# LRU gates in two matmul passes over blocks of 64 features, and attention gates earlier, in a hybrid decoder block

## The chip, the core and the metric

The kernel runs on one core of a Trainium2 chip. The core has a matrix engine (TensorE, in the profile PE), a vector engine (VectorE, DVE), a scalar engine for activation functions (ScalarE, ACT), a general engine (GpSimd, POOL) and SyncE (SP), whose queue here issues most transfers. Each engine runs its own instructions in order and waits for the others through semaphores. The metric is the time of one execution on the device in microseconds; less is better.

## The reference

One layer of a decoder block on 2048 positions of 1024 features, in float32. One projection gives everything: queries, keys and values of three groups of dilated attention, an attention gate, the input u_lru of a recurrent branch, its gate, and logits that merge both branches. The part that the change touches is the recurrent branch (RG-LRU) with its gates, which are block-diagonal: 16 blocks of 64 features, each with its own 64 x 64 matrix for r and for i.

```python
u = causal_depthwise_conv(u_lru, conv_w[l], conv_b[l])
...
xb = x.reshape(B, S, LRU_BLOCKS, LRU_BLOCK_WIDTH)
r = jax.nn.sigmoid((jnp.einsum('bsgi,gij->bsgj', xb, w_r).reshape(B, S, C) + b_r).astype(jnp.float32))
i = jax.nn.sigmoid((jnp.einsum('bsgi,gij->bsgj', xb, w_i).reshape(B, S, C) + b_i).astype(jnp.float32))
log_a = -LRU_C * r * jax.nn.softplus(-lam.astype(jnp.float32))
a = jnp.exp(log_a)
mult = jnp.sqrt(jnp.maximum(-jnp.expm1(2.0 * log_a), 0.0))
u = mult * (i * x.astype(jnp.float32))
...
_, h = lax.associative_scan(combine, (a, u), axis=1)
```

The attention's output is multiplied by silu(g_attn); silu(g_lru) multiplies h.

## The kernel before

**Stages.** The projection stage computes all projections together with rotary, the LRU branch and the gates, and stores the results in DRAM. Then come the attention stage, the combination of the groups, the output projections and the layer norm. Only the projection stage is touched.

**High and low parts.** A float32 value is kept as a high part in a rounded type (`F32R`, made by ACT with a copy) and the low rest (value minus high part, made by DVE or POOL). A product takes three matmul passes: high by high, high by low, low by high.

**Products and ticks.** The sequence is done in two halves of 1024 positions. In each half the list `seq` (line 534 on) gives 36 pairs of 128-feature tiles: `qk` (a key and a query tile), `ug` (LRU gate and LRU input), `v`, `ga` (attention gate), `mg` (merge gates). A pair is multiplied by a scheme with seven block products (the first pair of a half has eight plain ones). One product is 12 matmuls of 128x512 (`product`, line 590) and is one tick of the loop that writes out the instructions; a half has 8 + 35 x 7 = 253 ticks. Each engine's order is the order in which this loop writes. The raw weights, their sums, their high parts (L268) and low parts (L232) for a product are written three to four ticks ahead of it. In the first half DVE and POOL make the low parts and SP stores them in `wl_scr`; in the second half SP loads them back into the tiles `l` (`load_lo`, L290), of which there are four. A product's PSUM bank is one of four and is emptied by DVE or ACT (`evacuate`).

**Passage.** Shortly before the second half, x for its columns is loaded (`load_raw`, L226) by SP and combined on DVE, ACT and POOL (`comb`, `fourth`).

**Chains.** What follows a product runs as a chain, a generator that yields `Ask(...)` before each step. At each tick the loop steps every chain whose lag has passed, whose number of free tiles (`need` + `keep` of 32 slots) is there, and whose engines have budget left: a tick gives each engine 2.75 us, and an Ask's numbers (ACT=..., DVE=...) are taken off. So larger numbers in an Ask push later steps to later ticks. The chains: `qk_chain` (four swap transfers L310, products with cos and sin, their sum, for queries a split L333, stores L327, L338, L341), `v_chain` (four transposes on PE L358, a copy on ACT, store L370), `silu_chain` (two ACT, one DVE, L396 to L399; the attention gate is then stored, the LRU gate waits for h), `mg_chain`, and `lru`.

**The LRU chain** (`lru`, line 430) runs once per tile of 128 features (i, 8 of them) and chunk of 512 positions (c, 4 of them), 32 times. It does the convolution, and brings the gate weights twice per tile (`bring_gw`, 16 times): wr and wi as 128x128 block-diagonal matrices with two transfers into `gr` (L441, L442), then one high part on ACT (L459) and one low part on DVE. It splits v into vh and vl (L466 and L232), and has the six gate matmuls run in the middle of a later product (`pe_later`; L475 to L477: two banks `g`, three passes each). Two tanh (L488, L489) read the two banks; then follow exp, tanh, a square root, the products, the scan on DVE (L510), the product with the LRU gate on POOL and a store (L525). At most two chunks are between begin and scan (`gate["live"]`), and one between gates and tanh (`gate["busy"]`). For even i, chunk 1 is put off to the second half. So 12 chunks and 8 weight sets fall in the first half, 20 and 8 in the second.

**Order of the pairs.** The loop that makes `seq` takes from the list `light` (6 `v`, 2 `ga`, 6 `mg`): one behind an even tile's pair, two around an odd tile's.

## Time and profile before

| | |
|---|---|
| median of three runs | 2367.07 us (2362.84 to 2371.19) |
| profiled execution | 2367.64 us |
| its span, first to last instruction | 2365.8 us |
| granted TensorE clock, mean | 0.979 |
| PE, DVE, ACT, POOL busy | 95%, 73%, 46%, 43% |
| projection stage | 0 to 1546 us of the span |
| first half, second half | ticks 0 to 252, 253 to 505 |

How to read it: an engine's line such as `L605 PE MATMUL` names the kernel's line, the engine and the operation, then output<-input by tile names. A busy PE is an upper bound, because the records of neighbouring matmuls overlap. A wait is put down to the engine whose semaphore came last; `SPq` is SP's transfer queue. Line 232 is the helper `tt`, so the tile names tell what it does there. The program's built order, engine by engine, tells in which tick each instruction stands.

### The profile page before, as it was taken

How to read it: one execution, taken by the hardware profiler on the slowest of the kernel's cores; microseconds unless marked ns; L12 is line 12 of the kernel's file. 1: busy time of each engine (PE TensorE's matmuls, PEld its weight loads, DVE VectorE, ACT ScalarE, POOL GpSimd, SP SyncE). 2: the span in 40 equal slices, each digit the busy share in tenths (PEclk: the TensorE clock that was granted, in tenths of full speed). 3: DMA queues.
4: the chain of work that ended last, by engine and by line, in shares of the span. 5: the costliest groups of instructions: out<-in, count | busy, mean ns of one | idle time of the engine just before them, and what ended most of it. 6: DMA issues, size and time to landing. Idle time of an engine off the chain costs nothing.

```text
span 2365.8 us, 34610 instructions
## 1 busy us (share of the span) xinstructions
PE 2243.7 (95%) x11008; PEld 1878.5 (79%) x11008; DVE 1726.1 (73%) x3116; ACT 1084.9 (46%) x1977; POOL 1014.7 (43%) x760
## 2 busy tenths in 40 slices
PE   6999999999999799999999999989999999979998
PEld 4788888888788687787787877779999878758886
DVE  7888888899888676676667777546666558857677
ACT  4346445455465455465456665446666611121100
POOL 5554554456545433223232232368666326532220
PEclk8999999999999899999999999989999999999999
DMA  6888997988988987898897888897886579874431
GB/s 237 238 260 236 271 286 230 265 258 265 269 260 295 287 245 229 240 245 233 230 252 244 268 241 255 253 255 191 214 211 162 162 233 304 269 241 155 157 116 63
DMA packets 347174, 551.48 MB, mean 233 GB/s; under 512 B 99056, under 2 KB 140016, under 8 KB 342384
## 3 DMA queue, kind: packets, MB, share of 16 engines
q1 hardware_dynamic: 308160, 489.80, 66.2%
q0 software_dynamic: 20160, 36.71, 9.5%
q10 hardware_dynamic: 18672, 22.75, 3.1%
q8 instruction: 88, 1.44, 0.3%
q14 instruction: 94, 0.77, 0.1%
HBM read 343.81 MB, written 180.16 MB: 221 GB/s over the span
## 4 chain that ended last, share of the span: by engine, by line
PE 61%; DMA 13%; DVE 10%; issue 7%; POOL 4%; ACT 3%; SPq 2%; ACTq 0%; DVEq 0%; POOLq 0%
PE q L605 43%; DMA l<-wl_scr 4%; PE o L978 3%; PE s L939 2%; DMA A<-qh_scr 2%; PE pt L954 1%; PE yb L1167 1%; PE yb L1168 1%; PE yb L1166 1%; PE z L1260 1%; PE z L1258 1%; PE z L1259 1%; DVE xcB L232 1%; POOL C L789 1%; DMA wA<-in_w_in_dram 1%
## 5 line engine op out<-in xcount | busy, mean ns | idle before, releaser
L605 PE MATMUL q<-xT,hS 128*128 128x512 f32 x1680 | 523.3, 393 | 10.5 <-ACT hS L268 6.1
L605 PE MATMUL q<-xT,l 128*128 128x512 f32 x1120 | 438.9, 392 | 3.2 <-DVE l L232 3.2
L605 PE MATMUL q<-xB,hA 128*128 128x512 f32 x1248 | 398.7, 401 | 19.1 <-ACT hA L268 11.5
L605 PE MATMUL q<-xB,l 128*128 128x512 f32 x904 | 362.2, 401 | 36.8 <-DMA l<-wl_scr 28.2
L605 PEld LDWEIGHTS q<-xT,hS 128*128 128x128 f32 x1680 | 317.0, 189 | 78.7 <-ACT hS L268 7.1
L605 PEld LDWEIGHTS q<-xB,hA 128*128 128x128 f32 x1248 | 240.5, 194 | 70.6 <-ACT hA L268 12.3
L605 PEld LDWEIGHTS q<-xT,l 128*128 128x128 f32 x1120 | 211.7, 189 | 48.9 <-DVE l L232 4.3
L605 PEld LDWEIGHTS q<-xB,l 128*128 128x128 f32 x904 | 173.9, 192 | 81.4 <-DMA l<-wl_scr 35.1
L945 ACT ACTIVATE p<-p,osb 128x256 f32<-128x256 f32 (+1 forms) x384 | 156.5, 455 | 114.1 <-DVE osb L943 113.4
L232 POOL TENSOR_TENSOR sw<-sw,sin 128x512 f32<-128x512 f32 x96 | 159.8, 1681 | 98.6 <-DMA sw<-y 96.5
L943 DVE CUSTOM_DVE_ANT_0 p<-s,mask 128x256 f32<-128x256 f32 (+1 forms) x384 | 125.1, 364 | 100.4 <-PE s L939 59.6
L250 POOL DMA_DIRECT2D wS<-in_w_in_dram x140 | 123.8, 994 | 169.8 <-DMA wS<-in_w_in_dram 103.0
L268 ACT ACTIVATE hA<-wA 128x512 fp32r<-128x512 f32 x218 | 134.9, 623 | 95.3 <-DMA wA<-in_w_in_dram 51.1
L605 PE MATMUL q<-xB,hS 128*128 128x512 f32 x560 | 175.4, 394 | 2.1 <-DVE v L232 2.0
L605 PE MATMUL q<-xT,hA 128*128 128x512 f32 x560 | 174.1, 392 | 0.2 <-DVE u L232 0.2
L978 PE MATMUL o<-V,ptb 128*128 128x65 f32 x1200 | 165.0, 276 | 9.7 <-ACT ptb L959 7.8
L232 POOL TENSOR_TENSOR S<-S,wA 128x512 f32<-128x512 f32 x35 | 50.1, 1433 | 281.6 <-DVE S L232 116.3
L978 PEld LDWEIGHTS o<-V,ptb 128*128 128x128 f32 x1200 | 151.7, 194 | 21.4 <-ACT ptb L959 19.4
L232 DVE TENSOR_TENSOR y<-y,cos 128x512 f32<-128x512 f32 x96 | 121.3, 1267 | 48.6 <-DMA sw<-y 48.3
L232 POOL TENSOR_TENSOR l<-wA,hA 128x512 fp32r<-128x512 f32 x74 | 116.6, 1576 | 55.7 <-ACT hA L268 37.7
L1232 POOL TENSOR_TENSOR me<-gA,ybr 128x512 f32<-128x512 f32 x32 | 47.8, 1507 | 180.1 <-DVE gA L1231 177.6
L605 PEld LDWEIGHTS q<-xB,hS 128*128 128x128 f32 x560 | 104.3, 189 | 24.8 <-issue 2.9
(190 smaller groups left out, 4995.2 us busy)
## 6 DMA issues: line engine op xcount, KB each, us to landing
wA<-in_w_in_dram SPq DMA_DIRECT2D x218, 256.0 KB, 5.6
wl_scr<-l SPq DMA_DIRECT2D x105, 512.0 KB, 4.9
l<-wl_scr SPq DMA_DIRECT2D x105, 512.0 KB, 6.2
wS<-in_w_in_dram SPq DMA_DIRECT2D x140, 256.0 KB, 4.9
wS<-in_w_in_dram POOLq DMA_DIRECT2D x140, 256.0 KB, 7.0
sw<-y SPq DMA_DIRECT2D x384, 64.0 KB, 3.7
mg_scr<-y SPq DMA_DIRECT2D x59, 256.0 KB, 5.9
o_scr<-osb ACTq DMA_DIRECT2D x48, 264.0 KB, 5.9
```

The lines of the kernel that those rows point to most:

```text
L232: eng.tensor_tensor(out=out, in0=in0, in1=in1, op=op)
L250: pool.dma_start(t, w_part(s, x), accum_op=ALU.add)
L268: act.activation(h, r, AF.Copy)
L605: pe.matmul(bank, w[:, ks], x[:, kk, xx], start=(first and i == 0), stop=(last and i == 11))
L789: pool.tensor_tensor(out=b2[hs, h, t], in0=flat(b2[hs, h, t]), in1=flat(B1[hs, h, t]), op=ALU.subtract)
L939: pe.matmul(s[:, h, (0 if g == 2 and n else lo):256], q, k, start=(i == 0), stop=(i == 1))
L943: dve.tensor_tensor_reduce(out=p[:, h, lo:256], in0=s[:, h, lo:256], in1=mask[:, lo:256], scale=1.0, scalar=3e38, op0=ALU.add, op1=ALU.min ...
L945: act.activation(p[:, h, lo:256], p[:, h, lo:256], AF.Exp, scale=-1.0, bias=mm)
L954: pe.transpose(pt[:, 2 * h + x, :], p[:, h, x * P:(x + 1) * P], ident)
L978: pe.matmul(o[:, n % 2, h * 65:h * 65 + 65], ptb[:, 2 * h + x, :], V[:, kb, vo + h * 65:vo + h * 65 + 65], start=(x == lo // P), stop=(x = ...
L1166: pe.matmul(yb, WL[f][:, 0, k], xx[:, 0], start=(k == 0), stop=False)
L1232: pool.tensor_tensor(out=ME[c][:, f], in0=ga, in1=yb, op=ALU.add)
```

## The change

A tile of 128 features holds two gate blocks, b = 0 (rows 0 to 63) and b = 1 (rows 64 to 127). The changed kernel forms one matmul operand per block: the block's high part on its own rows and its low part on the other 64 rows of the same tile. So the first tile, still named vh, holds high and low of block 0, and vl holds those of block 1. The weights for block b have r and i beside each other in the 128 columns and the same 64 rows twice, below each other; a second such set holds their low parts. One pass with the high weights gives high by high plus high by low, a second pass with the low weights adds low by high (and low by low, which the kernel before left out). So a chunk has four gate matmuls instead of six. Bank 0 then has r and i of block 0 on its two halves, bank 1 has i and r of block 1, and each tanh becomes two of 64 partitions; the one for i moves its rows to the other half.

The pieces on ACT and DVE change so: the split of v from one to two instructions on each engine, a weight set from one to four on each, the tanh from two to four on ACT. The transfers of a weight set become four, of the 64x64 blocks alone (16 KB each), instead of two of 64 KB. Three Asks name larger numbers. In `light`, the two attention gate pairs come to the first and the fourth place instead of the seventh and eighth.

```diff
@@ lru, weights' transfers @@
-            sp.dma_start(gr[:, 0:P], a["wr"][i])
-            sp.dma_start(gr[:, P:2 * P], a["wi"][i])
+            for b, names in ((0, ("wr", "wi")), (1, ("wi", "wr"))):
+                for k, n in enumerate(names):
+                    rows = slice(64 * b, 64 * b + 64)
+                    sp.dma_start(gr[rows, 64 * k:64 * k + 64], a[n][i, rows, rows])
...
@@ weights' parts @@
-            yield Ask(ACT=.4, DVE=.4, lag=2, need=1, keep=1)
+            yield Ask(ACT=.9, DVE=.9, lag=2, need=1, keep=1)
             w = GW[i] = take("gw" + nm)
-            act.activation(w[:, 0:2 * P], gr[:, 0:2 * P], AF.Copy)
-            tt(dve, w[:, 2 * P:], gr[:, 0:2 * P], flat(w[:, 0:2 * P]), ALU.subtract)
+            for b in range(2):
+                rows, cols = slice(64 * b, 64 * b + 64), slice(2 * P * b, 2 * P * b + P)
+                low = slice(2 * P * b + P, 2 * P * b + 2 * P)
+                for o in (rows, slice(64 - 64 * b, P - 64 * b)):
+                    act.activation(w[o, cols], gr[rows, 0:P], AF.Copy)
+                    tt(dve, w[o, low], gr[rows, 0:P], flat(w[rows, cols]), ALU.subtract)
...
@@ split of v @@
-        gw = GW[i].rearrange("p (l j f) -> p l j f", l=2, j=2)
-        yield Ask(need=2, keep=1, ACT=.66, DVE=.75)
+        gw = GW[i].rearrange("p (b l f) -> p b l f", b=2, l=2)
+        yield Ask(need=2, keep=1, ACT=1.3, DVE=1.5)
         vh, vl = take("vh" + nm), take("vl" + nm)
-        act.activation(vh, v, AF.Copy)
-        tt(dve, vl, v, flat(vh), ALU.subtract)
+        for b, t in enumerate((vh, vl)):
+            rows, other = slice(64 * b, 64 * b + 64), slice(64 - 64 * b, P - 64 * b)
+            act.activation(t[rows], v[rows], AF.Copy)
+            tt(dve, t[other], v[rows], flat(t[rows]), ALU.subtract)
...
@@ gate matmuls @@
-                pe.matmul(g, gw[:, 0, j], vh, start=True, stop=False)
-                pe.matmul(g, gw[:, 0, j], vl, start=False, stop=False)
-                pe.matmul(g, gw[:, 1, j], vh, start=False, stop=True)
+                for l in range(2):
+                    pe.matmul(g, gw[:, j, l], (vh, vl)[j], start=(l == 0), stop=(l == 1))
...
@@ tanh @@
-        yield Ask(lag=2, need=3, keep=1, ACT=3.3, DVE=.75)
+        yield Ask(lag=2, need=3, keep=1, ACT=4.7, DVE=.75)
...
-        act.activation(tr, pg[0], AF.Tanh, scale=0.5, bias=brh[:, 0, i:i + 1])
-        act.activation(ti, pg[1], AF.Tanh, scale=0.5, bias=brh[:, 1, i:i + 1])
+        for t, k in ((tr, 0), (ti, 1)):
+            for b in range(2):
+                rows = slice(64 * b, 64 * b + 64)
+                src = rows if k == 0 else slice(64 - 64 * b, P - 64 * b)
+                act.activation(t[rows], pg[b][src], AF.Tanh, scale=0.5, bias=brh[rows, k, i:i + 1])
...
@@ order of the light pairs @@
-    light += [("ga", FT_GA + 2 * j, FT_GA + 2 * j + 1) for j in range(2)] + mg[2:]
+    for j in range(2):
+        light.insert(3 * j, ("ga", FT_GA + 2 * j, FT_GA + 2 * j + 1))
+    light += mg[2:]
```

## The prediction

> **What bounds the kernel now.** I read the page's first part, then busy time by stages, then what TensorE waited for in each stage, and then single instructions.
>
> ```profile
> span 2365.8 us, 34610 instructions
> PE 2243.7 (95%) x11008; PEld 1878.5 (79%) x11008; DVE 1726.1 (73%) x3116; ACT 1084.9 (46%) x1977; POOL 1014.7 (43%) x760
> ```
>
> The change touches the projection stage alone, so I cut the span there: the start, the first half of the sequence, the passage between the halves, the second half, and the rest (attention and output, untouched). Columns: window, its length, busy time and count of each engine, granted clock, DMA share, GB/s.
>
> ```profile
> 0.00:77.30 77.30, 50.51 (x169) 37.86 (x169) 59.75 (x83) 30.70 (x52) 39.72 (x38) 0.87 0.69 226
> 77.30:777.10 699.80, 696.60 (x3109) 574.15 (x3110) 610.93 (x721) 350.37 (x585) 374.16 (x275) 1.00 0.89 264
> 777.10:813.70 36.60, 23.50 (x85) 18.34 (x84) 23.12 (x28) 14.78 (x26) 15.65 (x12) 0.77 0.83 241
> 813.70:1546.10 732.40, 703.64 (x3073) 575.35 (x3072) 499.11 (x664) 404.45 (x660) 218.92 (x174) 0.98 0.86 247
> 1546.10:2365.80 819.70, 769.45 (x4577) 672.78 (x4575) 533.24 (x1623) 284.60 (x654) 366.21 (x263) 0.98 0.66 195
> ```
>
> In the first half PE is busy for 696.6 of 699.8 us while VectorE (DVE) has 610.9, or 87%: PE is the bound there and DVE is close behind. In the second half PE lacks 28.8 us. TensorE's own waits, asked for 130 to 700 us (first two rows), 700 to 820 and 820 to 1500, give the reasons:
>
> ```profile
> PE q L605 <- ACT hi L332: 1.6, 1, 1.6
> PE q L605 <- DVE v L232: 0.9, 2, 0.8
> ...
> PE q L605 <- ACT hA L268: 11.0, 1, 11.0
> ...
> PE q L605 <- DMA l<-wl_scr: 25.7, 13, 3.5
> ```
>
> So nearly nothing in the first half, one wait of 11 us in the passage, and 13 waits for the low weight parts coming back from memory in the second half. The gates appear in no wait of PE: their matmuls stand inside a product and cost their own time.
>
> **Term 1: 64 matmuls go.** The end of one product with the gates of one chunk in its middle, from the timeline of PE:
>
> ```profile
> 1307.48 0.39 PE L475 MATMUL g<-vh,gw 128*128 128x512 f32 x1
> 1307.71 0.39 PE L476 MATMUL g<-vl,gw 128*128 128x512 f32 x1
> ...
> 1308.84 0.61 PE L605 MATMUL q<-xT,hS 128*128 128x512 f32 x2
> ```
>
> Six gate matmuls fill 1307.48 to 1308.84, 1.36 us, or 0.227 us each; the 0.39 us of a record overlaps its neighbours, so the pitch is the price. Four remain per chunk. 32 chunks x 2 x 0.227 = 14.5 us less on PE: 12 chunks (5.4 us) stand before the passage in the built order, 20 (9.1 us) behind it. The matmuls keep their shape and partitions, so I expect the same pitch.
>
> **Term 2: more instructions on ScalarE (ACT) and DVE.** The groups, kept apart by shape:
>
> ```profile
> L232 DVE TENSOR_TENSOR vl<-v,vh 128x512 fp32r<-128x512 f32 x32 | 27.9, 872 | 13.4 <-ACT vh L466 7.8 <-DMA k_scr<-rp 5.1
> L232 DVE TENSOR_TENSOR gw<-gr,gw 128x256 fp32r<-128x256 f32 x16 | 8.4, 527 | 15.3 <-ACT gw L459 15.2
> L466 ACT ACTIVATE vh<-v 128x512 fp32r<-128x512 f32 x32 | 19.9, 623 | 13.5 <-DVE v L452 10.5 <-DMA k_scr<-rp 2.5 <-PE q L605 0.4
> L459 ACT ACTIVATE gw<-gr 128x256 fp32r<-128x256 f32 x16 | 6.6, 410 | 6.5 <-DMA gr<-in_wi_dram 6.0 <-DVE u L232 0.5
> L488 ACT ACTIVATE tr<-g,brh 128x512 f32<-128x512 f32 x32 | 21.9, 685 | 14.5 <-PE g L477 12.0 <-PE vtp L358 1.1 <-DMA mg_scr<-y 1.0
> L489 ACT ACTIVATE ti<-g,brh 128x512 f32<-128x512 f32 x32 | 21.9, 683 | 2.0 <-PE q L605 1.1 <-DVE h L510 0.9
> ```
>
> An instruction on 64 partitions isn't in this trace. From below it could cost half (nothing in these rows points to it), from above twice, if it is restarted. I take the time of the full tile with the same row length. For rows of 128 I go down the line through 512 and 256: DVE 527 - (872 - 527)/2 = 355 ns, ACT 410 - (623 - 410)/2 = 304 ns. Then DVE gets 32 more low-part subtractions, 27.9 us, and 64 x 0.355 - 8.4 = 14.3 us for the weights: 42 us, of which 17.6 in the first half (12 chunks, 8 weight sets). ACT gets 19.9 for the high parts, 43.8 for 64 more tanh, 64 x 0.304 - 6.6 = 12.9: 77 us over 1546. ACT has 350 of 700 and 404 of 732 us busy, so its share rises to some 55 to 61%: beside PE, price nothing. One wait gets tighter: both banks of g are now free only after the fourth tanh (4 x 0.685 = 2.7 us of ACT) instead of one after each. In the built order the next gates follow two ticks (5.4 us) behind the tanh, which leaves 2.7 us for what ACT has queued before them; past that PE itself waits, with the whole product behind the gates. I take nothing for it.
>
> DVE has less room. Where does its new work land? In the built order, the 14 ticks from 84 (277.7 us) get 9 DVE instructions more, the next 14 get 4 more:
>
> ```profile
> 277.70:319.50 41.80, 41.68 (x191) 34.05 (x190) 33.89 (x45) 25.47 (x44) 21.06 (x16) 1.00 0.94 269
> 319.50:357.60 38.10, 38.10 (x169) 31.53 (x168) 36.47 (x43) 16.46 (x30) 23.54 (x17) 1.00 0.92 280
> 559.80:619.70 59.90, 57.95 (x254) 47.02 (x253) 55.90 (x57) 22.03 (x40) 36.56 (x27) 1.00 0.94 278
> ...
> L399 DVE SCALAR_TENSOR_TENSOR y<-si,y 128x512 f32<-128x512 f32 x48 | 33.7, 704 | 3.2 <-ACT y L397 3.2
> L333 DVE SCALAR_TENSOR_TENSOR rp<-rp,hi 128x512 fp32r<-128x512 f32 x32 | 29.6, 927 | 2.6 <-ACT hi L332 2.3
> L232 DVE TENSOR_TENSOR rp<-y,sw 128x512 f32<-128x512 f32 x64 | 99.8, 1570 | 14.5 <-POOL sw L232 14.4
> ```
>
> The nine are one low part (0.87), three weight pieces net (4 x 0.355 - 0.527 = 0.89), four silu products of the attention gate that came forward (2.8) and one query split (0.93): 5.5 us. The next block gets 0.87 + 0.89 = 1.8. Together DVE goes from 70.4 to 77.7 us in 79.9 us, from which PE's own saving takes some 2: full. The same stands at ticks 28 to 55. What a nearly full DVE does to PE shows the third row: 55.9 of 59.9 us busy, and PE lost 2 us. Below: nothing, since the second row has DVE at 96% for 38 us and PE at 100%, the work being prepared three to four ticks (8 to 11 us) ahead. Above: the whole 17.6. I take the nearest row, 2 us at each of two places, less the 2 us at 560 to 620, where DVE gets relief since the attention gates have left the blocks ahead of it: +2.
>
> A rule of the Trainium skill speaks against the change here: VectorE: DVE Perf Modes, section "Two Vector instructions with no wait between them", says that an instruction whose input or output starts in another group of 32 partitions than the one before starts only when every earlier one has finished. The new pieces start at partition 0 and 64 in turn. The trace has no such start; what it would take away is the overlap of neighbours:
>
> ```profile
> 564.39 0.68 DVE L232 TENSOR_TENSOR y<-q,v 128x512 f32<-128x512 f32 x1
> 564.99 0.67 DVE L232 TENSOR_TENSOR l<-wS,hS 128x512 fp32r<-128x512 f32 x1
> ```
>
> Start to start is 0.60 us for records of 0.68, an overlap of 0.08. By that rule about three of four starts in a low-part pair or weight set would lose it, an estimate of 68 x 0.08 = 5.4 us of DVE in the first half, and the sum would be up to 5 us higher; I leave it out of the sum.
>
> **Term 3: the passage between the halves.** The longer gate chains meet a shortage of tiles at the end of the first half: by the built order four transfers of 256 KB (the two query parts, a key, an LRU result) slip from before tick 245 to ticks 245 to 247, in front of and among the loads of x for the second half. These stand in SP's queue and on the same DMA engines:
>
> ```profile
> 738.90:777.10 38.20, 38.20 (x169) 31.64 (x170) 29.87 (x34) 22.53 (x38) 26.01 (x18) 1.00 0.95 323
> ...
> qh_scr<-hi SPq DMA_DIRECT2D x48, 256.0 KB, 6.2
> k_scr<-rp SPq DMA_DIRECT2D x32, 256.0 KB, 4.4
> ```
>
> DMA is at 95% there, and PE then waits 11 us for what hangs on these loads. 4 x 0.262 MB at 323 GB/s = 3.2 us, later for every load behind them, so the wait grows. The two rope sums and two splits that slip with them (2 x 1.57 + 2 x 0.93 = 5.0 us) fit DVE's 8.3 us of room in that row: nothing, but if that cover is gone they add to the same wait. Below 0 (the loads may have spare time), above 6.2 (one store's landing in front of them); I take 3.2.
>
> **Term 4: SP's queue in the second half.** Why the low parts come late shows the queue in a block with rotary work (SP's DMA instructions from 1074 us):
>
> ```profile
> 1077.44 0.53 SPq L290 DMA_DIRECT2D l<-wl_scr  x1
> 1078.01 0.93 SPq L239 DMA_DIRECT2D wS<-in_w_in_dram  x2
> 1079.04 0.38 SPq L370 DMA_DIRECT2D v_scr<-vs  x1
> 1079.51 2.91 SPq L310 DMA_DIRECT2D sw<-y  x4
> 1082.53 0.53 SPq L370 DMA_DIRECT2D v_scr<-vs  x1
> 1083.15 2.41 SPq L310 DMA_DIRECT2D sw<-y  x4
> 1085.66 0.53 SPq L290 DMA_DIRECT2D l<-wl_scr  x1
> ...
> l<-wl_scr SPq DMA_DIRECT2D x105, 512.0 KB, 6.2
> ...
> L441 SPq DMA_DIRECT2D gr<-in_wr_dram x16: 333/638/4427, 121.8 to 1449.2; - x16
> ```
>
> One issue is 0.4 to 0.7 us, and the second load of l stands behind twelve others. With the change, the two v stores there become an LRU store and one of the attention gate, so the load keeps its place. The LRU store waits for POOL's product, which waits for DVE's scan; behind it stand eight swaps and that load. The weight loads of a gate set are four instead of two, 16 more issues in this half at about 0.5 us; in most blocks they stand behind the last urgent l load, at tick 431 in front of one. Below -3 (one wait less in each of two blocks), above +6 (the 13 waits each 0.5 longer); I take +0.5. The rest of PE's 9.1 us comes through, as swaps, stores and loads all follow PE's own ticks.
>
> **Sum.** -14.5 + 2 + 3.2 + 0.5 = -8.8 us. The profiled execution took 2367.64 us (span 2365.8), the median of three runs is 2367.07, so nothing has to be corrected: 2358.8 us.
>
> **The rivals.**
> - DVE becomes the bound of the first half, and the kernel is slower. Place: ticks 28 to 62 and 84 to 125; it decides as soon as DVE's lag passes the four ticks that weights and PSUM banks are ahead. Then all of its 17.6 us come out on PE, with 3.2 in the passage and 4 in the second half (13 waits, each 0.3 longer, since chains end later in front of SP): -14.5 + 24.8 = +10.3, 2378. For it: DVE full by the count above. Against it: DVE was at 96% for 38 us without harm, and the groups' sums count the overlap of neighbours twice. By the skill's rule above it would be 2383.
> - The second half's saving is hidden: its length is set by SP and DMA (86% busy) and the l waits grow by what PE saves. -5.4 + 2 + 3.2 = -0.2: 2367.4. For it: 13 waits. Against it: they sum to 25.7 of 732 us and lie in blocks whose triggers are PE's.
> - The early attention gates thin SP's queue so that the l waits of the two blocks at ticks 294 and 350 vanish: about 4 of 13 waits, 25.7 x 4/13 = 7.9 us: 2358.8 - 7.9 = 2351. For it: two issues fewer in each. Against it: the load itself keeps its place.
>
> **How the numbers follow.** Forecast 0.50, DVE bound 0.20, hidden 0.17, thinner queue 0.13. 0.3% is 7 us, about what a measurement of this kernel tells from no change: 2360 to 2374 counts as the same. The forecast lies 1 us beyond that bound, with its own range of 2350 (terms 2 and 3 nothing, term 4 -3) to 2367 (passage and queue at their upper bounds, 3.0 + 5.5 more): 0.33 faster, 0.17 same. The thin queue: all faster. Hidden: 0.02, 0.13, 0.02. DVE bound: 0.03 same, 0.17 slower. Faster 0.48, same 0.33, slower 0.19. The range runs from below the thin queue (2346) to the bound DVE (2378).
>
> **What would show it.** Gate matmuls x128 at a pitch of 0.227 us. Half-tile pieces near 0.87 and 0.355 us on DVE, 0.62, 0.30 and 0.68 on ACT; if they are half as long, DVE's term falls. The first half (ticks 0 to 252) 3 us shorter; waits of PE for DVE above 5 us there speak for the bound DVE. The passage's wait for hA at 14 rather than 11 us. The l waits within 23 to 32 us: if they reach 33, the saving was hidden. I am wrong if PE's time outside the gates rises, or if the attention stage, which nothing touches, begins later than its shift.

## The result, and the profile after

The changed kernel takes 2383.41 us (median of 4, 2381.47 to 2386.03), the kernel before 2364.95 (median of 4, 2360.47 to 2371.19). The ratio is 1.0079, with a 95% interval of 1.0054 to 1.0103: slower by 0.8%, some 19 us. The forecast of 2358.8 was wrong, and the time lies above its range of 2346 to 2378. The nearest case was the rival in which DVE becomes the bound of the first half.

The profiled execution of the changed kernel took 2381.47 us. The first part of its page, and its busy time in the first half, the passage and the second half (columns as in the prediction):

```profile
span 2379.4 us, 34781 instructions
...
PE 2236.7 (94%) x10944; PEld 1863.9 (78%) x10944; DVE 1756.0 (74%) x3196; ACT 1171.9 (49%) x2121; POOL 1022.4 (43%) x760
```

```profile
76.20:798.30 722.10, 700.51 (x3085) 569.56 (x3086) 631.65 (x756) 384.20 (x645) 377.54 (x274) 1.00 0.86 254
798.30:837.00 38.70, 23.24 (x85) 18.24 (x84) 23.85 (x27) 14.75 (x26) 17.45 (x13) 0.78 0.83 243
837.00:1558.50 721.50, 692.78 (x3033) 565.60 (x3032) 515.34 (x709) 457.73 (x744) 221.50 (x174) 0.99 0.88 250
```

Against the rows of before, the first half grew from 699.8 to 722.1 us, and there PE was without work for 21.6 us instead of 3.2. The second half shrank from 732.4 to 721.5. DVE's share of the first half is what it was: 631.65 of 722.10, 87%. So DVE isn't full over the half, and yet PE waits for it. The waits of TensorE show this (us in total, number of waits and the longest; the changed kernel's first half, its passage, its second half; the last row is the first half of before):

```profile
PE q L618 <- DVE u L232: 13.1, 10, 4.5
PE q L618 <- DVE v L232: 2.1, 3, 0.9
PE vtp L358 <- DVE y L564: 1.7, 3, 0.6
PE q L618 <- DVE y L564: 1.4, 2, 0.7
...
PE q L618 <- ACT hA L268: 13.1, 1, 13.1
...
PE q L618 <- DMA l<-wl_scr: 28.4, 18, 4.7
...
PE q L605 <- DVE u L232: 0.2, 1, 0.2
```

Ten waits for `u`, the step that empties a product's bank on DVE, add to 13.1 us; before it was one, of 0.2 us. The passage's wait grew from 11.0 to 13.1 us. The waits for l add to 28.4 us, as before (28.2 when the window of before begins behind its passage, too).

A finer cut goes by the products themselves: the time from the start of one tick's first matmul to that of another, in the profiled executions. Ticks 14 to 253 are the first half behind its start, 253 to 266 the passage, 266 to 505 the second half, and the rest goes to the end of the span. The experiments, which the next section describes, are read in this table too.

| kernel | first half | passage | second half | rest |
|---|---|---|---|---|
| before | 683.5 | 53.0 | 735.1 | 817.0 |
| changed | 704.5 | 56.4 | 724.2 | 818.2 |
| e1_order | 680.5 | 52.1 | 732.7 | 818.9 |
| e2_gates | 711.6 | 50.7 | 748.2 | 812.1 |
| e4_second | 682.1 | 53.7 | 733.9 | 813.7 |
| e5_asks | 681.5 | 54.8 | 710.6 | 815.5 |
| e3_pe | 681.4 | 54.5 | 722.7 | 811.6 |
| f5_pe | 682.3 | 53.0 | 706.1 | 814.3 |
| e8_tanh | 690.4 | 52.4 | 738.4 | 812.1 |
| e9_split | 686.2 | 50.7 | 734.6 | 816.1 |
| e10_gwpieces | 682.1 | 52.8 | 730.4 | 819.9 |
| f4_allpieces | 703.0 | 55.7 | 724.1 | 816.2 |
| f1_tanhwhole | 691.4 | 55.4 | 718.2 | 819.8 |
| f2_splitwhole | 697.9 | 53.4 | 721.8 | 814.6 |
| e7_weights | 703.3 | 56.8 | 746.8 | 820.4 |
| g1_transfers | 701.8 | 57.2 | 718.5 | 817.0 |
| g2_later | 699.7 | 57.2 | 720.2 | 813.4 |
| g3_both | 698.4 | 54.4 | 714.4 | 815.5 |
| g5_tanhlater | 701.4 | 58.6 | 735.3 | 816.7 |

For the change: +21.0, +3.4, -10.9 and +1.2, with 1.1 us less ahead of tick 14: the 13.6 us between the two spans. Each row is one execution, and that of before took 2367.64 us, where its medians beside the experiments are 2354.44 to 2362.90. e1_order, which the timing can't tell from before, differs from its row by 0.9 to 3.0 us in every column: differences of that size say nothing.

The growth of the first half isn't spread evenly. The products of ticks 77 to 83 take 24.6 us instead of 19.0 and those of ticks 133 to 139 take 25.4 instead of 19.0, 12 of the 21 us together.

**The new pieces.** Their groups in the changed kernel (projection stage; line, engine, operation, tiles, shape and count, then busy time and mean ns of one, then idle time in front):

```profile
L500 ACT ACTIVATE ti<-g,brh 64x512 f32<-64x512 f32 x64 | 43.8, 684 | 1.4
L500 ACT ACTIVATE tr<-g,brh 64x512 f32<-64x512 f32 x64 | 43.6, 681 | 4.4 <-PE g L485 2.2 <-DVE sq L232 1.0 <-DMA mg_scr<-y 0.4
L232 DVE TENSOR_TENSOR gw<-gr,gw 64x128 fp32r<-64x128 f32 x64 | 22.0, 344 | 9.9 <-ACT gw L466 9.0
L232 DVE TENSOR_TENSOR vh<-v,vh 64x512 fp32r<-64x512 f32 x32 | 21.9, 686 | 4.2 <-ACT vh L475 3.2
...
L475 ACT ACTIVATE vl<-v 64x512 fp32r<-64x512 f32 x32 | 20.2, 630 | 2.9 <-POOL S L232 1.8 <-DMA ql_scr<-rp 0.4
...
L466 ACT ACTIVATE gw<-gr 64x128 fp32r<-64x128 f32 x64 | 19.6, 306 | 6.2 <-DMA gr<-in_wi_dram 2.8 <-DMA gr<-in_wr_dram 2.2
```

Half the partitions take the whole time: 0.68 us for a half tanh, as for a whole one. Between neighbours more is lost than a group's mean tells. A tanh step on ACT, in the timeline of before and then of the changed kernel (an entry "x2" is two instructions in a row):

```profile
143.56 0.68 ACT L488 ACTIVATE tr<-g,brh 128x512 f32<-128x512 f32 x1
144.13 0.69 ACT L489 ACTIVATE ti<-g,brh 128x512 f32<-128x512 f32 x1
144.70 0.82 ACT L490 ACTIVATE e<-tr,sp2n 128x512 f32<-128x512 f32 x1
```

```profile
146.18 1.37 ACT L500 ACTIVATE tr<-g,brh 64x512 f32<-64x512 f32 x2
147.58 1.38 ACT L500 ACTIVATE ti<-g,brh 64x512 f32<-64x512 f32 x2
148.99 0.82 ACT L501 ACTIVATE e<-tr,sp2n 128x512 f32<-128x512 f32 x1
```

Before, the two tanh took 144.70 - 143.56 = 1.14 us from start to the start of what follows, 0.57 each. The four halves take 148.99 - 146.18 = 2.81 us, 0.70 each: they start at partitions 0 and 64 in turn and don't overlap any more (the last section has the test of that). DVE does the same with the halves of v's low part (137.67 to 138.39: 0.72, against 0.60 between whole tiles in the prediction's rows):

```profile
137.67 0.68 DVE L232 TENSOR_TENSOR vh<-v,vh 64x512 fp32r<-64x512 f32 x1
138.39 0.69 DVE L232 TENSOR_TENSOR vl<-v,vl 64x512 fp32r<-64x512 f32 x1
```

### The profile page after: what moved, and what is told of

The parts are those of the page before. It is cut to its first block, busy times and chain, and to the rows that moved or that the text cites. A ratio compares the mean times of both kernels' runs of the same rounds, so it can differ in the third digit from the quotient of the medians.

```text
span 2379.4 us, 34781 instructions
## 1 busy us (share of the span) xinstructions
PE 2236.7 (94%) x10944; PEld 1863.9 (78%) x10944; DVE 1756.0 (74%) x3196; ACT 1171.9 (49%) x2121; POOL 1022.4 (43%) x760
## 4 chain that ended last, share of the span: by engine, by line
PE 30%; DMA 13%; issue 6%; DVE 6%; ACT 3%; POOL 2%; SPq 1%; ACTq 0%; DVEq 0%; POOLq 0%
PE q L618 14%; PE o L991 4%; DMA l<-wl_scr 3%; PE s L952 3%; DMA A<-qh_scr 2%; PE pt L967 2%; PE z L1273 1%; PE z L1271 1%; PE z L1272 1%; POOL me L1245 1%; DMA oc<-o_scr 1%; PE yb L1180 1%; PE yb L1181 1%; PE yb L1179 1%; ACT p L958 1%
## 5 line engine op out<-in xcount | busy, mean ns | idle before, releaser
L618 PE MATMUL q<-xB,hA 128*128 128x512 f32 x1248 | 396.2, 399 | 21.4 <-ACT hA L268 13.1
L618 PE MATMUL q<-xB,l 128*128 128x512 f32 x904 | 361.2, 400 | 37.7 <-DMA l<-wl_scr 28.4
L618 PEld LDWEIGHTS q<-xB,hA 128*128 128x128 f32 x1248 | 240.1, 193 | 74.6 <-ACT hA L268 13.5
L232 POOL TENSOR_TENSOR sw<-sw,sin 128x512 f32<-128x512 f32 x96 | 158.6, 1671 | 61.9 <-DMA sw<-y 58.4
L232 POOL TENSOR_TENSOR S<-S,wA 128x512 f32<-128x512 f32 x35 | 55.6, 1588 | 292.3 <-DMA wA<-in_w_in_dram 103.6
L618 PEld LDWEIGHTS q<-xT,hA 128*128 128x128 f32 x560 | 107.6, 193 | 38.7 <-issue 16.1
```

Source lines behind the costliest of these rows:

```text
L232: eng.tensor_tensor(out=out, in0=in0, in1=in1, op=op)
L618: pe.matmul(bank, w[:, ks], x[:, kk, xx], start=(first and i == 0), stop=(last and i == 11))
```

## The experiments

Each was timed in three rounds beside the kernel before on the same chip; the ratio is to that kernel, with its 95% interval. 0.1% is 2.4 us. Line numbers in rows are those of the kernel named.

### What the change is made of: order, timetable, gates

**e1_order**: the attention gates come earlier, nothing else.

```diff
-    light += [("ga", FT_GA + 2 * j, FT_GA + 2 * j + 1) for j in range(2)] + mg[2:]
+    for j in range(2):
+        light.insert(3 * j, ("ga", FT_GA + 2 * j, FT_GA + 2 * j + 1))
+    light += mg[2:]
```

> The kernel before with one edit: the attention gate pairs stand first and fourth among the light pairs; gates and Asks as before. Theory 'work' (the added pieces on DVE and ACT make DVE late in the first half, and PE then waits for it): the order alone adds 4 DVE and 5 ACT instructions to ticks 28 to 41 and 84 to 97 and takes as many from ticks 140 to 182, so at most a few us: 2362 to 2371, within 0.3% of before, PE's waits for DVE in the first half under 6 us. Theory 'order' (the early gates overload these ticks): most of the loss is here already, 2375 or more, and the product at ticks 77 to 83 is long (24 us instead of 19).

Measured: 2358.07 against 2358.19 us, 0.9998 [0.9981, 1.0016]. The order alone moves nothing.

**e2_gates**: the changed kernel with the order and the three Asks of before (each back as here), so the two passes with all their pieces alone.

```diff
-        yield Ask(lag=2, need=3, keep=1, ACT=4.7, DVE=.75)
+        yield Ask(lag=2, need=3, keep=1, ACT=3.3, DVE=.75)
...
```

> The two-pass gates with the old order of the light pairs and the old numbers in the Asks. Theory 'work': still slower than before, first half 8 to 20 us longer, 2370 to 2382. Theory 'order': the loss is gone and the 14.5 us of PE show, 2350 to 2356. Theory 'Asks' (the larger numbers bunch the chains' steps): likewise 2350 to 2360.

Measured: 2404.03 against 2358.19 us, 1.0199 [1.0172, 1.0226]. By themselves the two passes cost 47 us, in both halves (first +28.1, second +13.1); that is more than any of the theories expected, and nothing of the 64 matmuls' gain is seen.

**e4_second**: the two passes, with the larger Asks, only in the second half; order of before.

```diff
+        late_half = c >= 2 or (c == 1 and i in put_off)
...
-        yield Ask(lag=2, need=3, keep=1, ACT=3.3, DVE=.75)
+        yield Ask(lag=2, need=3, keep=1, ACT=4.7 if late_half else 3.3, DVE=.75)
...
```

> Two passes in the 20 chunks of the second half alone, with their larger Asks; the first half's 12 chunks and the order of the light pairs as in the kernel before. Theory 'work': the first half is back at its length of before (ticks 0 to 252 within 2 us), the second keeps its gain of about 9 to 11 us: 2353 to 2359, faster than both. Theory 'order': the gain of the second half came from the early attention gates, which are not here: 2360 to 2368.

Measured: 2359.46 against 2358.19 us, 1.0011 [0.9993, 1.0029]. With the larger Asks the second half is as long with the two passes as before (733.9 us against 735.1), without the 9.1 us of 40 fewer matmuls: its waits for l rose from 28.2 to 36.0 us. Against before, the loss of the change lies in the first half; the next run shows what the second half loses against its own timetable.

**e5_asks**: the timetable alone. The gates of before, with the new order (as in e1_order) and the larger Asks.

```diff
-            yield Ask(ACT=.4, DVE=.4, lag=2, need=1, keep=1)
+            yield Ask(ACT=.9, DVE=.9, lag=2, need=1, keep=1)
...
-        yield Ask(need=2, keep=1, ACT=.66, DVE=.75)
+        yield Ask(need=2, keep=1, ACT=1.3, DVE=1.5)
...
-        yield Ask(lag=2, need=3, keep=1, ACT=3.3, DVE=.75)
+        yield Ask(lag=2, need=3, keep=1, ACT=4.7, DVE=.75)
```

> The kernel before (six gate matmuls, whole tiles) with the new order of the light pairs and the larger numbers in the Asks, so the timetable of the changed kernel without its pieces and with all gate matmuls. Theory 'work': the timetable costs nothing by itself, within 0.5% of before, and the first half (ticks 14 to 252) stays at 680 to 686 us; the loss of the changed kernel then lies in the pieces. Theory 'timetable': the later steps stand where DVE and SP are full; the first half takes 695 us or more, the whole 1% more than before.

Measured: 2339.82 against 2357.64 us, 0.9917 [0.9895, 0.9940]. It beats both kernels, by 0.8% and 1.6%, with six gate matmuls and whole pieces. Nearly all of the gain on before lies in the second half; the changed kernel is 23.0 us behind it in the first half and 13.6 in the second. The second half's window and waits for l of before, and then those of e5_asks:

```profile
813.70:1548.80 735.10, 706.34 (x3085) 577.61 (x3084) 499.80 (x665) 405.18 (x661) 221.48 (x176) 0.98 0.86 247
```

```profile
PE q L605 <- DMA l<-wl_scr: 28.2, 14, 3.5
```

```profile
812.50:1523.00 710.50, 695.63 (x3085) 571.57 (x3084) 495.88 (x664) 406.11 (x661) 220.10 (x176) 1.00 0.89 255
```

```profile
PE q L607 <- DMA l<-wl_scr: 14.8, 10, 3.3
```

PE's time without work falls from 28.8 to 14.9 us, and the same 3085 matmuls take 10.7 us less, since the granted clock goes from 0.98 to 1.00 (see the last section). The Ask's larger numbers push LRU steps to later ticks; which of the queued transfers the load of l is freed from wasn't taken apart, and the Asks weren't tried in the old order for both halves.

### What the 64 matmuls are worth

**e3_pe** takes the kernel before, **f5_pe** e5_asks; both leave the third pass out.

```diff
-                pe.matmul(g, gw[:, 0, j], vl, start=False, stop=False)
-                pe.matmul(g, gw[:, 1, j], vh, start=False, stop=True)
+                pe.matmul(g, gw[:, 0, j], vl, start=False, stop=True)
```

> The kernel before with four gate matmuls instead of six: the pass of the low weights by the high part of v is left out of the gates; nothing else changes. All theories: PE's 64 matmuls go and nothing is added, so 14.5 us less if nothing else bounds the stage: 2350 to 2354. Theory 'hidden' (the second half's length is set by SP and DMA): only the first half's 5.4 us, about 2360.

> The gates of before in the changed kernel's timetable (new order of the light pairs, larger Asks), with four of the six gate matmuls (the pass with the low parts of the weights is left out). 64 matmuls fewer than the timetable alone, which stood at 0.9917. Theory 'full pitch': 64 x 0.227 = 14.5 us less, ratio 0.985 to 0.986. Theory 'partly hidden', as in the timetable of before where the same cut gave 8 us: ratio 0.988 to 0.990.

Measured: e3_pe 2352.78 against 2358.19 us, 0.9967 [0.9947, 0.9988], 8 us. f5_pe 2336.25 against 2362.90 us, 0.9893 [0.9866, 0.9920], 0.24 points or 6 us below e5_asks. So 6 to 8 us came of the 14.5, loosely: the interval of e3_pe is 3 to 13 us, and that of f5_pe overlaps the one of e5_asks. In f5_pe the first half gained nothing (682.3 us against 681.5), and PE's waits there are 3 us more, 2 of them for DVE. The gain is in the second half (706.1 against 710.6).

### What the pieces cost

Each kind of piece alone in the kernel before: **e8_tanh** halves the two tanh, **e9_split** the split of v, **e10_gwpieces** cuts each weight part in four. All pieces stay within their own partitions.

```diff
@@ e8_tanh @@
-        act.activation(tr, pg[0], AF.Tanh, scale=0.5, bias=brh[:, 0, i:i + 1])
-        act.activation(ti, pg[1], AF.Tanh, scale=0.5, bias=brh[:, 1, i:i + 1])
+        for t, k in ((tr, 0), (ti, 1)):
+            for b in range(2):
+                rows = slice(64 * b, 64 * b + 64)
+                act.activation(t[rows], pg[k][rows], AF.Tanh, scale=0.5, bias=brh[rows, k, i:i + 1])
@@ e9_split @@
-        act.activation(vh, v, AF.Copy)
-        tt(dve, vl, v, flat(vh), ALU.subtract)
+        for b in range(2):
+            rows = slice(64 * b, 64 * b + 64)
+            act.activation(vh[rows], v[rows], AF.Copy)
+            tt(dve, vl[rows], v[rows], flat(vh[rows]), ALU.subtract)
@@ e10_gwpieces @@
-            act.activation(w[:, 0:2 * P], gr[:, 0:2 * P], AF.Copy)
-            tt(dve, w[:, 2 * P:], gr[:, 0:2 * P], flat(w[:, 0:2 * P]), ALU.subtract)
+            for b in range(2):
+                rows = slice(64 * b, 64 * b + 64)
+                for o in range(2):
+                    hi_, lo_c = slice(P * o, P * o + P), slice(2 * P + P * o, 3 * P + P * o)
+                    act.activation(w[rows, hi_], gr[rows, hi_], AF.Copy)
+                    tt(dve, w[rows, lo_c], gr[rows, hi_], flat(w[rows, hi_]), ALU.subtract)
```

> The kernel before with each of the two tanh over a gate bank in two halves of 64 partitions (64 more ACT instructions, 44 us of ACT by their durations), with the same order on PE and SP. Theory 'DVE' (the loss comes from pieces on DVE): no change, within 0.3%. Theory 'ACT queue' (weights' high parts stand behind the longer tanh steps in ACT's queue, and DVE and POOL wait for them): 10 to 25 us slower, with PE's waits for DVE or ACT in the first half above 8 us.

> The kernel before with the split of v in two pieces of 64 partitions on each engine (32 more on ACT, 32 more on DVE), same order on PE and SP. Theory 'DVE': 12 x 0.72 = 9 us of DVE more in the first half and 14 in the second, of which half or more comes out on PE: 5 to 20 us slower. Theory 'ACT queue': under 6 us.

> The kernel before with each weight set's high and low part in four pieces of 64 partitions and 128 columns on each engine (48 more on ACT, 48 more on DVE), same order on PE and SP. Theory 'DVE': 16 x (4 x 0.30 - 0.42) = 12 us of DVE, half of it in the first half: 3 to 8 us slower. Theory 'ACT queue': ACT gets 15 us more in single bursts of 1.3 us; 0 to 5 us slower.

Measured, against 2357.64 us: e8_tanh 2372.51, 1.0058 [1.0040, 1.0076]; e9_split 2364.86, 1.0025 [1.0009, 1.0042]; e10_gwpieces 2361.65, 1.0011 [0.9990, 1.0033], which can't be told from nothing. The tanh halves are work for ACT alone, an engine half idle, and by the medians they cost most (their interval just touches that of e9_split).

**f4_allpieces**: e5_asks with all three kinds of pieces, cut as in these three.

> The timetable of the changed kernel (new order, larger Asks, six gate matmuls) with all three kinds of pieces, each within its own 64 partitions: tanh in halves, v split in halves, weights in quarters. Theory 'pieces add up' (each costs what it cost alone: 15 + 7 + 4 us): about 26 us above the timetable alone (2340), 2362 to 2370. Theory 'pieces compound' (together they push ACT and DVE past what the lead of three to four ticks covers): 40 us or more above it, 2380 or more, so that the changed kernel's loss is all here. Theory 'crossing' (moving rows to the other 64 partitions is dear): under 2365, and the changed kernel stays 15 us or more above it.

Measured: 2371.47 against 2359.57 us, 1.0044 [1.0025, 1.0063]: 1.27 points, 30 us, above the timetable alone. Alone the three cost 0.94 points together; the intervals don't tell whether they only add up. The first half takes 703.0 us instead of 681.5, nearly the 704.5 of the changed kernel, and the second 724.1 instead of 710.6.

**f1_tanhwhole** and **f2_splitwhole** take one kind out of the changed kernel: the two whole tanh of before, or the whole split of v.

```diff
@@ f1_tanhwhole @@
-        for t, k in ((tr, 0), (ti, 1)):
...
+        act.activation(tr, pg[0], AF.Tanh, scale=0.5, bias=brh[:, 0, i:i + 1])
+        act.activation(ti, pg[1], AF.Tanh, scale=0.5, bias=brh[:, 1, i:i + 1])
@@ f2_splitwhole @@
-        for b, t in enumerate((vh, vl)):
...
+        act.activation(vh, v, AF.Copy)
+        tt(dve, vl, v, flat(vh), ALU.subtract)
```

> The changed kernel with two whole tanh in place of four halves; the sorting of r and i between the banks is left out. Theory 'ACT queue' (the tanh halves are the largest cost, through the weights' high parts behind them): 20 us or more faster than the changed kernel, so about the kernel before or below it (ratio 0.99 to 1.00). Theory 'DVE' (the pieces on DVE are): at most 8 us faster, ratio 1.005.

> The changed kernel with v split as before, one whole instruction on each engine; the swap of high and low parts between the blocks' tiles is left out. Theory 'DVE' (22 us of DVE go): 15 us or more faster than the changed kernel, ratio 1.00 or less. Theory 'ACT queue': 5 to 12 us faster, ratio 1.003 to 1.006.

Measured, against 2359.57 us: f1_tanhwhole 2359.81, 0.9990 [0.9975, 1.0006]; f2_splitwhole 2371.86, 1.0050 [1.0034, 1.0067]. Without the tanh halves the changed kernel is 0.89 points (21 us) faster and level with before; without the split's, 0.29 points (7 us), with intervals that overlap.

### How the tanh halves cost it

In VectorE's queue the product with v (`ti`) waits for the four tanh, and what stands behind it waits with it. Its waits in the first half, of before and of the changed kernel:

```profile
DVE ti L493 <- ACT ti L489: 1.4, 3, 0.5
```

```profile
DVE ti L504 <- ACT ti L500: 12.8, 7, 2.1
```

**g2_later** gives that product to VectorE one tick later, **g5_tanhlater** the second tanh's halves too.

```diff
-        dve.scalar_tensor_tensor(out=ti, in0=ti, scalar=1.0, in1=v, op0=ALU.add, op1=ALU.mult)
-        give(v)
+        def times_v():
+            dve.scalar_tensor_tensor(out=ti, in0=ti, scalar=1.0, in1=v, op0=ALU.add, op1=ALU.mult)
+            give(v)
+
+        later(1, times_v)
@@ g5_tanhlater: the same, and in times_v ahead of the product @@
+            halves(ti, 1)
```

> The changed kernel, but the product with v behind the tanh is given to VectorE one product later (at the head of the next tick), so that VectorE doesn't stand behind ScalarE's four tanh; nothing else moves. Theory 'in order' (the halves of tanh cost what VectorE loses in waiting for them, with the evacuations and low parts queued behind): VectorE's waits for ti fall from 12.8 us to 3 or less in the first half, and the kernel gets 8 us or more faster, ratio to before at most 1.004. Theory 'ScalarE itself' (what is late is ScalarE's own work behind the tanh: high parts, evacuations, splits): the waits for ti fall, but the time moves by less than 4 us, ratio 1.006 to 1.010.

> The changed kernel, but the two halves of the second tanh (for i), and the product with v behind them, are given one product later than the two halves of the first, so that ScalarE has two bursts of 1.4 us in place of one of 2.8; its work stays the same. Theory 'burst' (what stands behind four tanh in a row on ScalarE, high parts and evacuations above all, comes 1.4 us late and VectorE with it): 6 us or more faster than the changed kernel, ratio to before at most 1.005, TensorE's waits for u in the first half below 9 us (13 in the changed kernel). Theory 'amount' (ScalarE and VectorE wait for each other in turn, and any work added to that loop counts wherever it stands): within 4 us, ratio 1.006 to 1.010, waits for u 10 to 15 us.

Measured: g2_later 2373.96 against 2362.90 us, 1.0065 [1.0036, 1.0093]; g5_tanhlater 2387.70 against 2354.44 us, 1.0139 [1.0120, 1.0159]. In g2_later VectorE's waits for ti are all but gone, and TensorE waits for u as before that; VectorE waits elsewhere instead:

```profile
PE q L622 <- DVE u L232: 12.1, 12, 3.3
```

```profile
DVE l L232 <- ACT hA L268: 27.2, 16, 4.1
DVE S L232 <- DMA wA<-in_w_in_dram: 10.3, 7, 4.3
DVE nw L514 <- POOL l L232: 8.8, 3, 3.0
...
DVE ti L506 <- issue: 1.3, 3, 0.4
```

So VectorE's standing in line is not the main cause: some 3 us hang on it by the ratios, whose intervals overlap (its row in the table is the lowest of eight executions). With two bursts (g5_tanhlater) the waits for u fall to 7.4 us and the first half shrinks by 3 us, but the waits for l go to 35.1, and the kernel is 0.60 points (14 us) slower than the changed one. Neither of its theories expected that: the one on bursts forecast a gain, the one on the amount of work no change.

One explanation that is left is that ScalarE and VectorE hold each other up. ScalarE's spare time shows as its wait for PE's product behind the copy `e`, the first step that empties a bank. In the first half, before; the changed kernel; the timetable alone; without the tanh halves (with the product later it is 15.4 us in 4 waits); and e2_gates:

```profile
ACT e L628 <- PE q L605: 58.4, 14, 10.1
```

```profile
ACT e L641 <- PE q L618: 11.7, 2, 9.8
```

```profile
ACT e L630 <- PE q L607: 48.5, 17, 11.9
```

```profile
ACT e L638 <- PE q L615: 22.3, 8, 11.9
```

```profile
ACT e L639 <- PE q L616: 39.2, 10, 9.4
```

ScalarE is busy 53% of the changed kernel's first half, but it is hardly ever ahead of PE. Among the kernels with the new timetable this wait and the first half go together: 48.5 us with 681.5, 22.3 with 691.4, 11.7 with 704.5. With the old timetable they don't: e2_gates keeps 39.2 us of it and e8_tanh 46.9, and yet their first halves grew to 711.6 and 690.4. So the wait tells that ScalarE fell behind, but it is no measure of the loss.

Two other readings fit as well. VectorE's work between ticks 14 and 253 grew from 600.2 to 621.8 us, as much as the half itself (21.0), and its time without work stayed at 83 us, of which it waited 37 for ScalarE before and 48 after: a VectorE that sets the pace would look like this. It isn't its work alone, since f1_tanhwhole has as much (625.4 us) in 691.4 us. And SP's transfers take part. The two longest waits for u, 3.7 and 4.5 us, stand at ticks 83 and 139, in the long stretches of the result section. Ahead of both, VectorE had stood 2.5 and 3.3 us for the swap transfers of a key or query tile. Such waits were there before too (2.9 and 1.8 us), without a wait of PE, so they are on the path, but not shown to be the cause. The later place:

```profile
447.85 0.69 DVE L232 TENSOR_TENSOR y<-y,cos 128x512 f32<-128x512 f32 x1 [3.27 <-DMA sw<-y]
...
451.80 0.67 DVE L232 TENSOR_TENSOR u<-e,q 128x512 f32<-128x512 f32 x1
```

```profile
452.62 1.10 PE L618 MATMUL q<-xT,hA 128*128 128x512 f32 x2 [4.52 <-DVE u L232]
```

So it is shown that the tanh halves cost 21 us, by taking them out (alone, in e8_tanh, it was 14 us); how they come to cost it is not shown. That each added microsecond counts wherever it stands in the loop of ScalarE, VectorE and the transfers is how I read the runs. None of them shows it, since no kernel took the same work to another engine, and g5_tanhlater, with the same work, is 14 us slower.

### The transfers of the weights

**e7_weights** brings each weight set with eight transfers (the blocks already twice, below each other), and then needs only one piece on ACT and one on DVE: 96 pieces fewer. **g1_transfers** goes back to the two transfers of before, with the pieces reading from there (and r and i now stand in the same order in both banks). **g3_both** is g1_transfers with g2_later.

```diff
@@ e7_weights @@
-                    sp.dma_start(gr[rows, 64 * k:64 * k + 64], a[n][i, rows, rows])
+                    for o in range(2):
+                        sp.dma_start(gr[64 * o:64 * o + 64, P * b + 64 * k:P * b + 64 * k + 64], a[n][i, rows, rows])
...
@@ g1_transfers @@
-            for b, names in ((0, ("wr", "wi")), (1, ("wi", "wr"))):
-                for k, n in enumerate(names):
-                    rows = slice(64 * b, 64 * b + 64)
-                    sp.dma_start(gr[rows, 64 * k:64 * k + 64], a[n][i, rows, rows])
+            sp.dma_start(gr[:, 0:P], a["wr"][i])
+            sp.dma_start(gr[:, P:2 * P], a["wi"][i])
...
```

> The changed kernel with each weight block brought by two transfers into both halves of the raw tile (eight transfers of 16 KB a set instead of four), so that a set's high and low part are one instruction each on ACT and DVE; all results the same. 48 fewer instructions on each engine (15 us of ACT, 14 of DVE), 64 more transfers on SP's queue. Theory 'DVE': 5 to 12 us faster than the changed kernel, ratio 1.003 to 1.006. Theory 'SP queue' (64 issues of 0.5 us make the low parts later): no gain or slower, ratio 1.008 or more, l waits above 30 us.

> The changed kernel, but a weight set comes with the two transfers of 64 KB of before instead of four of 16 KB; its four pieces on each engine, the crossing of halves, the four matmuls and the timetable stay. Theory 'SP queue' (the four transfers cost it): 8 to 12 us faster than the changed kernel, ratio to before at most 1.004, the waits of TensorE for l in the second half below 24 us (28 in the changed kernel). Theory 'crossing' (pieces whose input and output lie in different partitions cost it, the transfers nothing): as the changed kernel, 1.007 to 1.010, l waits 26 to 31 us.

> The changed kernel with both earlier alterations: two transfers of 64 KB per weight set as before, and the product with v one product later. If each acts by itself, their gains in the profiled executions (8.4 us with the transfers, 12.9 us with the product, of which only 4.8 us in the first half where VectorE's wait went) partly add: 1.002 to 1.005. If the second half is what gains (waits of TensorE for l, 28 us in the changed kernel, 24 and 26 in the two), these waits fall below 23 us and the first half stays within 3 us of the later product's alone.

Measured: e7_weights 2399.70 against 2359.57 us, 1.0165 [1.0137, 1.0192]; g1_transfers 2374.57 against 2362.90, 1.0049 [1.0030, 1.0068]; g3_both 2367.24 against 2354.44, 1.0053 [1.0036, 1.0070]. The changed kernel's issues, and the waits for l in the second half with two transfers per set, which with four were 28.4 us:

```profile
L445 SPq DMA_DIRECT2D gr<-in_wr_dram x32: 473/594/3592, 122.3 to 1465.4; - x32
```

```profile
PE q L617 <- DMA l<-wl_scr: 23.6, 16, 3.3
```

With eight they were 45.1 us (21 waits), in g3_both 22.7. A transfer of 16 KB takes as long to issue as one of 64 KB (median 0.594 us against 0.638), so the count is the price: doubling it costs 0.86 points (20 us) in spite of fewer pieces. Halving it saved 8.4 us in the profiled spans and 0.30 points in the ratios. That lies between the two theories and the intervals overlap, but the waits for l fell as the SP queue's theory said. The crossing of halves wasn't run by itself; g1_transfers, which has it and 64 matmuls fewer, is level with f4_allpieces, so the crossing, or the weights' pieces in it, may hold the matmuls' 6 to 8 us. A part of it shows in the traces: the four weight pieces take 1.30 us on ACT where they cross and 1.02 where they don't (last section), 4.5 us for 16 sets, and some 3 us more on DVE. What that is worth stays open, as does the ratio's lack of any further gain in g3_both (its profiled span, 2358.9 us, is one low execution of four).

## Why the prediction was wrong

- **Term 2 failed**, the step "beside PE, price nothing" for ACT and "+2" for DVE. The durations were right: 0.68, 0.63 and 0.306 us on ACT against 0.685, 0.62 and 0.30; 0.344 us on DVE against 0.355; only v's low halves took 0.686 instead of 0.87. (The trace before does hold instructions on 64 partitions, but POOL's alone, L787 to L789.) Measured cost of the pieces: 30 us (f4_allpieces less e5_asks, by the ratios; in the profiled executions 37, of which 21.5 in the first half and 13.5 in the second). The largest part are the tanh halves that I priced at nothing: without them the changed kernel is 21 us faster. A share of busy time was read as room. The prediction didn't ask what the two engines wait for. In the first half ACT waited 58.4 us for PE's product before `e`, of which 11.7 are left, and DVE's waits for PE in the kernel before, 9.6 us in all, were less than the 17.6 us of work that it was to get. How the lost time runs through ACT, DVE and SP's transfers stays open (above).
- **The tighter wait for g** ("I take nothing for it"): right. PE's waits for g are in no row of the changed kernel; they appear when the tanh is put off (g5_tanhlater, 3.7 us) and, once, with the Asks of before (e2_gates, 3.0 us).
- **Term 1 was mis-sized.** The four gate matmuls run at the pitch forecast: 1486.75 to 1487.65, 0.225 us each, in these rows:

```profile
1486.75 0.62 PE L485 MATMUL g<-vh,gw 128*128 128x512 f32 x2
1487.20 0.62 PE L485 MATMUL g<-vl,gw 128*128 128x512 f32 x2
1487.65 0.61 PE L618 MATMUL q<-xT,hS 128*128 128x512 f32 x2
```

  But by e3_pe and f5_pe only 6 to 8 us came of 14.5, none of it clearly in the first half. I read this so that "PE is the bound there" held only for a PE as slow as it was; the pace is then set by ACT and DVE.
- **Term 3, the passage**: +3.2 forecast, +3.4 by ticks, the wait for hA 13.1 us instead of 14. The number was met, the mechanism isn't shown: e5_asks, with the same order there, has +1.8, and e1_order, with nothing changed there, a wait for hA of 9.0 us. No run moved the four transfers by themselves.
- **Term 4, SP's queue**: +0.5 forecast. The 32 more issues cost some 7 us by g1_transfers, whose interval overlaps that of the changed kernel, and of the ticks' gain there 5.7 us lie in the second half; the direction was right and the size too small. The price was taken from one issue's 0.5 us, not from what stands behind it when the queue is already late.
- **What the sum lacked**: the timetable's own gain, 0.83 points or 20 us, in the waits for l. The Asks are part of the change, but no step prices them. The rival of the thinner queue gave the early attention gates 7.9 us of it; e1_order shows that they bring nothing alone. Because this gain and the new cost cancel, the waits for l came out "within 23 to 32 us", as forecast for another reason: 28.2, then 14.8 by the timetable, 24.3 with the pieces (f4_allpieces) and 28.4 with the transfers too. That it fell into the range is luck.
- **The rival "DVE becomes the bound"** had the sign and nearly the place: PE's waits for DVE in the first half, 18.3 us, pass its mark of 5. But its ticks 28 to 62 and 84 to 125 grew by 2.6 and 1.1 us only; the growth came right behind them, 6.8 us in ticks 62 to 84 and 7.3 in 125 to 140. Whether its reason, a full DVE, holds stays open: the share is 87% before and after, but the half grew by as much as DVE's work did. Its 2378, or 2383 by the skill's rule, met the time by terms that differ from its own: -20 timetable, +30 pieces, and +8 as what remains, for matmuls, transfers and crossing together (in ratios -0.83, +1.27 and +0.35 of the measured 0.79 points).
- **The rival "the second half's saving is hidden"** is not seen where only matmuls went: in e3_pe the waits for l stayed at 28.1 us (28.2 before) and the second half got shorter. With the pieces (e4_second) they rose to 36.0.
- **The rule that was left out of the sum** (the Trainium skill, VectorE: DVE Perf Modes, section "Two Vector instructions with no wait between them"): the trace agrees, with 0.72 us between halves that start at other partitions and 0.60 between whole tiles. The prediction doesn't say how its 68 starts are counted: 12 chunks with two low parts and 8 weight sets with four pieces have 56, and three of four of them are 42, or 3.4 us. Even the 5 us are a quarter of the 21 us lost in the first half, so with it the forecast would still have been wrong, but a rule that bears on every new piece belonged into the sum.

## What to carry to other kernels

A low share of busy time is not room: ScalarE was half idle, and 64 half tanh more cost 21 us. Before an engine is given more work, ask what its idle time waits for, and take only its waits for the bounding engine as possible room; what stands beside them here (e2_gates) shows that even they can be left while the kernel gets slower. Halving an instruction over partitions saves nothing (0.68 us for a half tanh and for a whole one) and so doubles its cost; a saving on TensorE that is paid with such halves must be larger than what they add on the other engines and in waits. When a change also moves a timetable, build the timetable alone first: here it was the part that paid.

## What the runs showed of the hardware

**ScalarE too loses the overlap** between neighbours that start at other partitions: 0.70 us from start to start for halves of tanh against 0.57 for whole ones, in the rows shown with the result. That it is the start and not the half shows a weight set's four pieces of 64x128, in e10_gwpieces and in the changed kernel:

```profile
347.56 1.02 ACT L463 ACTIVATE gw<-gr 64x128 fp32r<-64x128 f32 x4
```

```profile
360.07 1.30 ACT L466 ACTIVATE gw<-gr 64x128 fp32r<-64x128 f32 x4
```

In e10_gwpieces two pieces in a row stay on the same 64 partitions and start 0.20 to 0.22 us apart, and only the third starts on the other 64, 0.32 us behind the second. In the changed kernel each start moves, and all are 0.32 to 0.33 us apart. VectorE's four take 1.00 and 1.18 us.

**A wait of TensorE costs more than itself.** Behind a wait for l in the kernel before, the timeline of PE shows the pitch of the matmuls (three in two rows) change:

```profile
1094.18 0.50 PE L605 MATMUL q<-xB,l 128*128 128x512 f32 x1 [2.19 <-DMA l<-wl_scr]
...
1096.17 1.05 PE L605 MATMUL q<-xB,hA 128*128 128x512 f32 x2
1097.02 0.63 PE L605 MATMUL q<-xB,l 128*128 128x512 f32 x1
1097.45 1.05 PE L605 MATMUL q<-xT,hA 128*128 128x512 f32 x2
...
1100.24 0.62 PE L605 MATMUL q<-xT,hA 128*128 128x512 f32 x2
1100.70 0.39 PE L605 MATMUL q<-xT,l 128*128 128x512 f32 x1
1100.93 0.62 PE L605 MATMUL q<-xB,hS 128*128 128x512 f32 x2
```

From 1096.17 three matmuls take 1.28 us, 0.427 each, and from 1100.24 again 0.69, 0.23 each. About eight run so slowly, some 1.6 us more for a wait of 2.2. Counting matmuls whose successor starts 0.38 to 0.47 us later, the second half has 49 before, 16 in e5_asks and 41 in the changed kernel, or 9.7, 3.2 and 8.1 us; this is most of what e5_asks gained beside the waits themselves. The Trainium skill, TensorE: Matmul & The Clock Gate, section Part 1, says that the clock falls to half after an idle window of about 3.4 us and is released after about 3.4 us of work. The trace agrees with the release (0.427 against 0.227 us, eight times: 3.4 us; the granted clock stands at half for 3.41 us from 1095.57 on) but not with the fall: here a wait of 2.2 us was enough.
